# Moving matmul operands to other SBUF address remainders in a Mamba-2 mixer

## The chip, the cores and the metric

The kernel runs on one core of one Trainium2 chip. The metric is the device time of one execution in microseconds, of which the median over several runs is given. A profiled execution has a time of its own; its span is the time from its first to its last instruction.

## The reference, cut to what matters

One layer: RMSNorm of x (512 tokens, 2048 channels), a Mamba-2 mixer, a residual add and a final RMSNorm.

```python
proj = rmsnorm(x, ln_g) @ w_in             # 2048 -> 4096 z, 6144 x/B/C, 64 dt
xbc = silu(causal_depthwise_conv(xbc, conv_w, conv_b))
y = ssd_chunked_scan(xs * dt, dt * a, bm, cm) + d_skip * xs
y = rmsnorm(y * silu(z), norm_g)
out = rmsnorm(x + y @ w_out, final_g)      # 4096 -> 2048
```

Everything is float32, and most of the time goes into the two projections.

## The kernel before, in words

**Splitting.** TensorE works in a rounded float32. Each operand is therefore cut into a rounded high part and a low part (the rest), and a product is three matmuls: high by high, low by high, high by low. A weight piece is loaded from HBM (load_piece, line 78), ScalarE writes its high part (line 87) and VectorE its low part (line 88).

**Plain products.** The first eight output streams of the input projection are computed directly, in mm_k (lines 194 to 199). The weights are stationary. x in its high and low part is the moving operand, in two halves of 256 tokens. xh and xl hold all of x: 16 blocks of 128 channels by 512 tokens each, 32,768 bytes per partition. The squares of x and the splits of x run beside this.

**Quads.** The other 72 streams are taken in pairs, 36 quads, by a Strassen-like scheme with seven products in place of eight. It adds and subtracts quarters of the weights and of x. The quarters of the weights are combined by a DMA that adds (q_fetch) and by VectorE (q_add, line 604). The quarters of x are made once. Forms 1, 2 and 4 lie in the twelve tiles s0 to s11 (x_forms). Forms 11, 3, 12 and 22 are read from xh and xl in place, the second halves after x_form3 has rewritten them. operand() says where a form lies. product() (lines 627 to 636) issues the 24 matmuls of a product: line 634 high by high, 635 low part of x, 636 low part of the weights. pair() sets the order of the products: 11, 1, the 22 of the quad before, 4, 2, 12, 3.

**The scan.** Between the products TensorE also does the small float32 matmuls and transposes of the scan (lines 416 to 520), hung on steps of the matmul order in a table of events (ev). VectorE does the convolution and gating and ScalarE the exponentials. One quad in five is for the group matrices B and C, so the work repeats in groups of five quads. The results y go to HBM (yscr).

**Output projection.** Half of the blocks of w_out go directly (mm_o, lines 911 to 917): y is stationary and the weights are the moving operand, 512 columns. The others go in two groups by the same seven-product scheme: y_forms (lines 816 to 845) makes seven forms of y, each in a high and a low tile, f11h, f11l and so on; oproduct (lines 849 to 861) multiplies them. There the form of y is stationary and the weights are the moving operand. Line 859 is high by high, 860 the low part of y, 861 the low part of the weights. At the end the tiles of the seven forms are used a second time: last_piece (lines 940 to 946) puts seven of the last eight weight pieces into them, and the last loop (from line 1036) reads these as moving operands.

**Order of work.** The order on TensorE, SyncE and GpSimd is as written. ScalarE and VectorE are ordered by the tile framework, which also places the waits.

**Addresses.** The pools are stacks in each partition, handed out in steps of 32 bytes. The pools on the right side grow down from byte 229,344, and a tile "edge" of 32 bytes that holds nothing is their first. Below it lies the pool of x, 114,688 bytes, until the input projection is over: xh at 114,624, xl at 147,392, the twelve s tiles from 180,160 on. All of these leave the remainder 192 modulo 256. In the same place then comes the pool op: acc at 114,432, further tiles, and from 171,840 on the fourteen tiles of the seven forms, 4,096 bytes each, all at remainder 64. Two tiles that hold nothing, "gap" of 64 bytes ahead of them and "gap1" of 128 bytes behind them, shift them there. The weight tiles hi, lo, h1h and h1l on the left side, oh and ol, and the direct pieces of y (ya, yb, yc) are at remainder 0.

Of the kernel before, what the change touches and what calls it, by code (L numbers as in the profile page):

```python
# [10 lines left out]
F32 = mybir.dt.float32  # L11
F32R = mybir.dt.float32r
# [5 lines left out]
P = 128  # L18
L = 512
DM = 2048  # L20
KT = DM // P
# [13 lines left out]
def mamba_layer(ctx: ExitStack, tc: tile.TileContext, d: dict, out: bass.AP):  # L35
# [19 lines left out]
    xp = phx.enter_context(tc.tile_pool(name="xhat", bufs=1, side="right"))  # L55
# [23 lines left out]
    def load_piece(src, shape, name="ra"):  # L79
        raw = wp.tile(shape, F32, name=name, bufs=RB[name])  # L80
        nc.sync.dma_start(raw, src)
        return raw
# [42 lines left out]
    OSH = [P, 2, L]  # L125
# [12 lines left out]
    QSH = [P, 4, LH]  # L138
# [6 lines left out]
    def wo_src(p, s):  # L145
        return d["wo"][p // 2, s, :, p % 2 * 2:p % 2 * 2 + 2, :]
# [16 lines left out]
                                     *((op, ("oh", "ol")) if n % 4 == 3 else (wp,)))  # L163


    xh = xp.tile([P, KT, L], F32R, name="xh")
    xl = xp.tile([P, KT, L], F32R, name="xl")
    SSH = [P, 4, LH]
    xr = sp.tile([P, L + 48], F32, name="xr")

# [632 lines left out]
    yform = {}  # L803
# [3 lines left out]
    def y_fetch(i, j):  # L807

        yraw[i, j] = n1, n2 = [op.tile([P, 2, L], F32, name="yr", bufs=2) for _ in range(2)]
        for n, g in zip((n1, n2), oquads[i]):  # L810
            nc.sync.dma_start(n, yscr[g][:, 2 * j:2 * j + 2, :])
            for k in range(2):
                kk = 4 * g + 2 * j + k
                S.activation(n[:, k, :], n[:, k, :], AF.Identity, scale=ng[:, kk:kk + 1])

    def y_forms(i, j):

        n1, n2 = yraw.pop((i, j))
        if j == 0:
            if i == 0:  # L820
                op.tile([P, 16], F32, name="gap")
            for f in YF:
                yform[i, f] = [op.tile(QSH, F32R, name=f"f{f}{c}") for c in "hl"]
            if i == 0:
                op.tile([P, 32], F32, name="gap1")
        jj = slice(2 * j, 2 * j + 2)
        t = fp.tile([P, 2, 2, LH], F32, name="yt")
        t1, t2 = t[:, 0], t[:, 1]

        def put(f, t):  # L830
            hi, lo = [x[:, jj, :] for x in yform[i, f]]
            S.copy(out=hi, in_=t)
            V.tensor_tensor(out=lo, in0=t, in1=hi, op=ALU.subtract)

        put(11, n1[:, :, lo_])
        V.tensor_tensor(out=t1, in0=n2[:, :, hi_], in1=n1[:, :, hi_], op=ALU.subtract)
        put(1, t1)
        V.scalar_tensor_tensor(out=t2, in0=t1, scalar=-1.0, in1=n1[:, :, lo_], op0=ALU.mult, op1=ALU.subtract)
        V.tensor_tensor(out=n1[:, :, hi_], in0=n1[:, :, lo_], in1=n1[:, :, hi_], op=ALU.subtract)
        V.scalar_tensor_tensor(out=t1, in0=t2, scalar=-1.0, in1=n2[:, :, lo_], op0=ALU.mult, op1=ALU.subtract)  # L840
        put(4, t1)
        put(2, t2)
        put(12, n2[:, :, lo_])
        put(3, n1[:, :, hi_])
        put(22, n2[:, :, hi_])

    YF = (11, 1, 4, 2, 12, 3, 22)

    def oproduct(ps, i, w, f, first, step):

# [89 lines left out]
    def last_piece(i):  # L940

        raw = load_piece(wo_src(14 + i % 2, i // 2), OSH)
        hi, lo = [op.tile(OSH, F32R, name=f"f{YF[i]}{c}" if i < 7 else "o" + c) for c in "hl"]
        S.copy(out=hi, in_=raw)
        V.tensor_tensor(out=lo, in0=raw, in1=hi, op=ALU.subtract)
        wlast.append((hi, lo))

    m = 0
    for i, blk in enumerate(blocks):
        if type(blk) is tuple:  # L950
            for s in range(4):
                q_events(len(quads) + 4 * m + s, base[i] + s * QS, s == 3, 0, 3 if s == 0 else 0)
            for j in range(2):
                add(base[i] - ((50, 32), (54, 32))[m][j], y_fetch, m, j)
                add(base[i] - ((39, 24), (47, 24))[m][j], y_forms, m, j)
            m += 1
# [6 lines left out]
    for i in range(7):  # L963
        add(base[4] - QS + 5 + 5 * i, last_piece, i)
# [16 lines left out]
    op = ctx.enter_context(tc.tile_pool(name="op", bufs=1, side="right"))  # L981
# [5 lines left out]
    for kb, blk in enumerate(blocks[:-1]):  # L987
# [8 lines left out]
        for s, pairs in blk:  # L996
            ps = [None] * NC
            for p in pairs:
# [4 lines left out]
                for t in range(NC):  # L1003
# [8 lines left out]
                    if p == pairs[-1]:  # L1012
                        a = acc[:, t, s * L:(s + 1) * L]
# [19 lines left out]

    assert not ev, ev
    last_piece(7)
    for t in range(NC):
        ss = fp.tile([P, 4], F32, name="ss", bufs=2)
        for s in range(4):
            ps = ps_o.tile([P, L], F32, name="mm")
            for i in range(2):  # L1040
                mm_o(ps, wlast[2 * s + i], ys[14 + i], t, i == 0, i == 1)
            a = acc[:, t, s * L:(s + 1) * L]
# [4 lines left out]
                            op=ALU.mult)  # L1047
# [6 lines left out]
        n = 2 if t < NC - 1 else 4  # L1054
        for i in range(n):
            c = slice(i * (DM // n), (i + 1) * (DM // n))
# [41 lines left out]
```

## Time and profile before

| | |
|---|---|
| median of 3 runs | 1301.98 us (1300.03 to 1308.32) |
| profiled execution | 1302.64 us |
| its span | 1300.9 us, 24461 instructions |
| mean granted TensorE clock | 0.993 |
| moved by DMA | 225.90 MB, mean 174 GB/s |

How to read it: a row of a group names the line, the engine and the operation, output and inputs with their shapes and the count; then the total busy time in us and the mean of one in ns; then the idle time of the engine just before, with what ended it. The mean of a matmul is that of its whole passage through the pipelined array, so neighbouring matmuls overlap, and the distance from start to start is shorter than the mean. PE is TensorE's matmuls, PEld its weight loads. A view by stages gives the length of each stretch, then the busy time and count of each engine, the clock, the share of the DMA engines and GB/s.

### The profile page before, as it was taken

Reading aid. Unit: us, or ns where it says so; the run is one execution under the profiler, and the core shown is the slowest. Engines: PE = TensorE matmul, PEld = TensorE weight load, DVE = VectorE, ACT = ScalarE, POOL = GpSimd, SP = SyncE. Lnnn points to the kernel's source line nnn. Section 1 sums busy time; section 2 is a strip of 40 time slices with the busy share of each in tenths; the row PEclk is TensorE's granted clock in tenths of the full one; section 3 lists DMA queues with packets and bytes.
Section 4 is the critical chain, followed back from the end, with each engine's and each line's share of the span. In section 5 each row is a group of like instructions: output and inputs, shape, how many; then the busy total and the mean of one; then the engine's idle time right before and its main releaser. Section 6 shows DMA issues by size and latency. Waiting matters only on the chain.

```text
span 1300.9 us, 24461 instructions
## 1 busy us (share of the span) xinstructions
PE 1250.4 (96%) x9932; PEld 1188.6 (91%) x9932; DVE 1082.3 (83%) x1449; ACT 827.6 (64%) x1357; POOL 77.7 (6%) x99
## 2 busy tenths in 40 slices
PE   8989999999999999999999999999899899999997
PEld 7989899999999999999999999999888799789885
DVE  5796888989988998988899899889856887878865
ACT  7667667578666857766785777668655444534523
POOL 0000001010100101010000101010000000001000
PEclk9999999999999999999999999999999999999998
DMA  9546657575685667567566656756636677658612
GB/s 357 174 143 184 173 146 173 154 193 141 188 207 156 165 168 182 146 184 209 156 158 192 158 158 180 218 143 154 185 107 205 201 181 221 197 130 220 201 42 98
DMA packets 70194, 225.90 MB, mean 174 GB/s; under 512 B 8384, under 2 KB 12800, under 8 KB 69952
## 3 DMA queue, kind: packets, MB, share of 16 engines
q1 hardware_dynamic: 56688, 176.34, 40.5%
q0 software_dynamic: 12672, 46.14, 21.4%
q8 instruction: 78, 1.28, 0.4%
q10 hardware_dynamic: 720, 1.84, 0.4%
q14 instruction: 36, 0.29, 0.1%
HBM read 211.52 MB, written 12.78 MB: 172 GB/s over the span
## 4 chain that ended last, share of the span: by engine, by line
PE 59%; DVE 15%; DMA 11%; ACT 8%; issue 6%; SPq 0%; POOL 0%; DVEq 0%; ACTq 0%; POOLq 0%
PE S L636 5%; PE S L634 5%; PE S L635 5%; PE mm L859 3%; PE mm L634 3%; PE mm L860 3%; PE mm L915 3%; PE mm L861 3%; PE mm L917 3%; PE mm L916 3%; PE R L634 3%; PE R L635 3%; PE R L636 3%; DMA ra<-in_wi 3%; DVE lo L88 3%
## 5 line engine op out<-in xcount | busy, mean ns | idle before, releaser
L88 DVE TENSOR_TENSOR lo<-ra,hi 128x1024 fp32r<-128x1024 f32 x150 | 180.7, 1220 | 55.9 <-ACT hi L87 55.7
L87 ACT CAST hi<-ra 128x1024 fp32r<-128x1024 f32 x150 | 154.7, 1047 | 85.7 <-PE mm L860 19.7
L634 PE MATMUL mm<-xh,hi 128*128 128x256 f32 x576 | 163.8, 284 | 0.0
L634 PE MATMUL R<-s,hi 128*128 128x256 f32 x576 | 160.7, 279 | 2.6 <-ACT sn L656 2.6
L87 ACT CAST hi<-rc 128x1024 fp32r<-128x1024 f32 x94 | 98.4, 1047 | 101.0 <-DMA rc<-in_wi 58.5
L636 PE MATMUL mm<-xh,lo 128*128 128x256 f32 x576 | 160.7, 279 | 0.3 <-DVE lo L88 0.3
L635 PE MATMUL mm<-xl,hi 128*128 128x256 f32 x576 | 160.6, 279 | 0.0
L636 PE MATMUL R<-s,lo 128*128 128x256 f32 x576 | 160.2, 278 | 0.0
L635 PE MATMUL R<-s,hi 128*128 128x256 f32 x576 | 160.2, 278 | 0.0
L604 DVE TENSOR_TENSOR ra<-ra,rc 128x1024 f32<-128x1024 f32 x88 | 107.4, 1220 | 33.9 <-DMA rc<-in_wi 33.5
L88 DVE TENSOR_TENSOR lo<-rc,hi 128x1024 fp32r<-128x1024 f32 x94 | 114.5, 1218 | 0.9 <-ACT hi L87 0.8
L634 PEld LDWEIGHTS mm<-xh,hi 128*128 128x128 f32 x576 | 108.4, 188 | 5.1 <-issue 5.0
L634 PEld LDWEIGHTS R<-s,hi 128*128 128x128 f32 x576 | 108.2, 188 | 3.4 <-ACT sn L656 3.4
L636 PEld LDWEIGHTS mm<-xh,lo 128*128 128x128 f32 x576 | 109.3, 190 | 0.5 <-DVE lo L88 0.5
L636 PEld LDWEIGHTS R<-s,lo 128*128 128x128 f32 x576 | 109.0, 189 | 0.0
L635 PEld LDWEIGHTS mm<-xl,hi 128*128 128x128 f32 x576 | 108.5, 188 | 0.1
L635 PEld LDWEIGHTS R<-s,hi 128*128 128x128 f32 x576 | 108.2, 188 | 0.0
L634 PE MATMUL S<-xh,hi 128*128 128x256 f32 x288 | 81.4, 282 | 9.8 <-ACT sn L670 7.5
L636 PE MATMUL S<-xh,lo 128*128 128x256 f32 x288 | 82.2, 285 | 4.3 <-DVE lo L88 4.3
L634 PE MATMUL S<-xh,h1h 128*128 128x256 f32 x288 | 83.3, 289 | 1.0 <-ACT mm L676 1.0
L635 PE MATMUL S<-xl,hi 128*128 128x256 f32 x288 | 80.3, 279 | 0.7 <-DVE xl L578 0.7
L635 PE MATMUL S<-xl,h1h 128*128 128x256 f32 x288 | 80.6, 280 | 0.0
(452 smaller groups left out, 3929.2 us busy)
## 6 DMA issues: line engine op xcount, KB each, us to landing
rc<-in_wi SPq DMA_DIRECT2D x76, 512.0 KB, 5.3
ra<-in_wi SPq DMA_DIRECT2D x42, 512.0 KB, 6.1
rb<-in_wi SPq DMA_DIRECT2D x40, 512.0 KB, 7.5
ra<-in_wi POOLq DMA_DIRECT2D x36, 512.0 KB, 7.7
rb<-in_wi POOLq DMA_DIRECT2D x36, 512.0 KB, 6.4
csb<-cscr SPq DMA_DIRECT2D x32, 512.0 KB, 8.7
ra<-in_wo SPq DMA_DIRECT2D x26, 512.0 KB, 5.2
yscr<-xs SPq DMA_DIRECT2D x32, 256.0 KB, 2.7
```

What stands on the lines that cost most here:

```text
L87: S.copy(out=hi, in_=raw)
L88: V.tensor_tensor(out=lo, in0=raw, in1=hi, op=ALU.subtract)
L604: V.tensor_tensor(out=raw, in0=raw, in1=qs[n][other], op=ALU.add)
L634: T.matmul(ps, hi[:, k, :], ah, start=first and k == 0, stop=False, skip_group_check=True)
L635: T.matmul(ps, hi[:, k, :], al, start=False, stop=False, skip_group_check=True)
L636: T.matmul(ps, lo[:, k, :], ah, start=False, stop=k == KH - 1, skip_group_check=True)
L859: T.matmul(ps[:, t, :], yh[:, k, tt], hi[:, k, :], start=st, stop=False, skip_group_check=True)
L860: T.matmul(ps[:, t, :], yl[:, k, tt], hi[:, k, :], start=False, stop=False, skip_group_check=True)
L861: T.matmul(ps[:, t, :], yh[:, k, tt], lo[:, k, :], start=False, stop=en, skip_group_check=True)
L915: T.matmul(ps, yh, hi, start=first and k == 0, stop=False)
L916: T.matmul(ps, yh, lo, start=False, stop=False)
L917: T.matmul(ps, yl, hi, start=False, stop=last and k == 1)
```

## The change

xh and xl become one tile of 65,568 bytes, 32 more than both. Each half lies 16 bytes behind the place it would have at the tile's start. The tile starts at 114,592 (remainder 160), so both halves leave the remainder 176; the s tiles stay where they were. Each form of y becomes one tile for its high and its low part. Six of the seven tiles are 32 bytes longer, with an inner offset of 16 bytes (8 bytes for form 2); form 4 has none. gap and gap1 are taken out. The pool op keeps its size, so the other tiles stay. The forms start at 171,776 (remainder 0) and leave the remainders 16, 48, 64, 72, 112, 144 and 176 in the order f11, f1, f4, f2, f12, f3, f22. In the last stage the weight pieces in these tiles have the same remainders. No instruction is added or removed.

```diff
-    xh = xp.tile([P, KT, L], F32R, name="xh")
-    xl = xp.tile([P, KT, L], F32R, name="xl")
+    xhl = xp.tile([P, 2 * KT * L + 8], F32R, name="xh")
+    xh, xl = [xhl[:, i * KT * L + 4:(i + 1) * KT * L + 4].rearrange("p (k l) -> p k l", k=KT) for i in range(2)]
...
+    def y_tile(f, shape):
+        n, o = shape[1] * shape[2], YF[f]
+        t = op.tile([P, 2 * n + (8 if o else 0)], F32R, name=f"f{f}")
+        return [t[:, i * n + o:(i + 1) * n + o].rearrange("p (a b) -> p a b", a=shape[1]) for i in range(2)]
...
         if j == 0:
-            if i == 0:
-                op.tile([P, 16], F32, name="gap")
             for f in YF:
-                yform[i, f] = [op.tile(QSH, F32R, name=f"f{f}{c}") for c in "hl"]
-            if i == 0:
-                op.tile([P, 32], F32, name="gap1")
+                yform[i, f] = y_tile(f, QSH)
...
-    YF = (11, 1, 4, 2, 12, 3, 22)
+    YF = {11: 4, 1: 4, 4: 0, 2: 2, 12: 4, 3: 4, 22: 4}
...
-        hi, lo = [op.tile(OSH, F32R, name=f"f{YF[i]}{c}" if i < 7 else "o" + c) for c in "hl"]
+        hi, lo = y_tile(list(YF)[i], OSH) if i < 7 else [op.tile(OSH, F32R, name="o" + c) for c in "hl"]
```

## The prediction, on record before the result

> **What bounds the kernel now.** I read the page first: the busy shares and the chain that ended last.
>
> ```profile
> span 1300.9 us, 24461 instructions
> PE 1250.4 (96%) x9932; PEld 1188.6 (91%) x9932; DVE 1082.3 (83%) x1449; ACT 827.6 (64%) x1357; POOL 77.7 (6%) x99
> PE 59%; DVE 15%; DMA 11%; ACT 8%; issue 6%; SPq 0%; POOL 0%; DVEq 0%; ACTq 0%; POOLq 0%
> ```
>
> TensorE is nearly always busy, yet the chain that set the end runs on it for only 59%; the rest is feeding. The change adds and removes no instruction, so it can only act through what one matmul costs. So I went to the timeline of TensorE in two quads of the x stage, first and last row of twelve matmuls in a row.
>
> ```profile
> 309.92 0.28 PE L634 MATMUL R<-s,hi 128*128 128x256 f32 x1
> ...
> 311.21 0.28 PE L636 MATMUL mm<-xh,lo 128*128 128x256 f32 x1
> ...
> 331.74 0.28 PE L634 MATMUL R<-s,hi 128*128 128x256 f32 x1
> ...
> 332.98 0.28 PE L636 MATMUL R<-s,lo 128*128 128x256 f32 x1
> ```
>
> From start to start it is 1.29 us / 11 = 117 ns in the first stretch and 1.24 us / 11 = 113 ns in the second, at the same remainders: moving operand at 192 modulo 256, weights at 0. In the first stretch the moving tile changes from the form s to xh without a change of pitch. So there are **two paces**, and remainder alone does not choose. The view by stages, restricted to line 635, tells them apart over whole quads (columns: stretch, length, TensorE busy and count, weight-load busy and count, clock, DMA):
>
> ```profile
> 304.90:327.60 22.70, 15.73 (x56) 10.52 (x56) 1.00 0.64 158
> 327.60:349.70 22.10, 15.47 (x56) 10.52 (x56) 1.00 0.70 197
> 643.30:666.00 22.70, 15.73 (x56) 10.52 (x56) 1.00 0.65 176
> 666.00:688.10 22.10, 15.48 (x56) 10.52 (x56) 1.00 0.64 172
> 869.70:892.40 22.70, 15.73 (x56) 10.52 (x56) 1.00 0.65 165
> 892.40:914.50 22.10, 15.47 (x56) 10.52 (x56) 1.00 0.74 182
> ```
>
> A slow quad has 15.73/56 = 280.9 ns per matmul, a fast one 276.3; the 4.6 ns are about the difference of the paces, and I use **4.5 ns** per matmul. The clock is 1.00 in all, so it is no throttle. The same quad of three different groups takes the same pace: what a stretch runs at is settled when TensorE starts again after another kind of work, and then it holds. The rows of all such matmuls give the mix:
>
> ```profile
> L635 PE MATMUL R<-s,hi 128*128 128x256 f32 x576 | 160.2, 278 | 0.0
> L635 PE MATMUL mm<-xl,hi 128*128 128x256 f32 x576 | 160.6, 279 | 0.0
> L198 PE MATMUL mm<-xl,hi 128*128 128x256 f32 x96 | 19.1, 280 | 0.0
> ```
>
> (160.2 + 160.6)/1152 = 278.5 ns, so (278.5 - 276.3)/4.6 = **about 0.47 of the x products run slow**; of the early plain products (line 198) about 0.8. For the output stage, line 860 by stages:
>
> ```profile
> 1017.20:1026.60 9.40, 6.74 (x24) 4.60 (x24) 1.00 0.39 60
> 1039.20:1094.90 55.70, 45.22 (x164) 30.72 (x164) 1.00 0.67 177
> ```
>
> 280.8 ns in the first, 275.7 in the second: slow at the entry, fast for the long rest; I call 0.15 of it slow.
>
> **The change part by part.** *Addresses.* Worked out from the tiles' sizes, xh and xl go from remainder 192 to 176 while the twelve form tiles of x stay at 192. The output's forms go from 64 to 16 (f11), 48 (f1), 64 (f4), 72 (f2), 112 (f12), 144 (f3), 176 (f22). acc, ya, hi, lo and the rest do not move. The two tiles gap and gap1 hold no work: 0 us.
>
> *One tile in place of two.* The high and low part now become free together, so a reallocated f tile waits for the later of the two last readers. In oproduct these are line 861 (high part) and line 860, one matmul earlier: at most 0.1 us for the low part, which waits for ScalarE's high part in any case. In last_piece the same:
>
> ```profile
> L945 DVE TENSOR_TENSOR f11l<-ra,f11h 128x1024 fp32r<-128x1024 f32 x1 | 1.2, 1227 | 0.1
> L945 DVE TENSOR_TENSOR f2l<-ra,f2h 128x1024 fp32r<-128x1024 f32 x1 | 1.2, 1218 | 0.0
> ```
>
> The wait stands on VectorE ahead of the next split, whose reader is a matmul some products later; 0 us. For xh and xl the last reader is the high part's, line 636 of the last product: 0 us.
>
> *VectorE and ScalarE at odd places.* xr is read and written 12 bytes past a boundary of 32 already, so the rows show what such a start costs them:
>
> ```profile
> L398 DVE TENSOR_TENSOR xr<-mm,rbc 128x512 f32<-128x512 f32 x39 | 26.8, 688 | 18.7 <-PE mm L636 15.7 <-PE mm L198 2.9
> L681 DVE TENSOR_TENSOR z<-z,rbc 128x512 f32<-128x512 f32 x30 | 20.5, 683 | 0.2
> L577 ACT CAST xh<-xr 128x512 fp32r<-128x512 f32 x4 | 2.5, 618 | 1.9 <-DVE xr L576 1.8
> L832 ACT CAST f12h<-yr 128x512 fp32r<-128x512 f32 x4 | 2.5, 618 | 0.0
> ```
>
> 688 ns against 683 (one reads PSUM, the other does not) and 618 against 618: 5 ns at most for each of some 90 splits, 0.5 us, hidden since TensorE reads the result later. I take 0.
>
> *TensorE's paces.* No matmul of this kernel that counts in the sum has an operand at 16, 48, 72, 112, 144 or 176, so this cost is bounded from both sides by the two paces.
> - x products: 36 quads of 7 x 24 matmuls, 6048. All fast saves 6048 x 0.47 x 4.5 ns = 12.8 us of TensorE; all slow costs 6048 x 0.53 x 4.5 = 14.4. Four of seven products read the moved halves; since a pace carries over from tile to tile, I let the bound hold all.
> - Plain products: 8 x 16 x 6 = 768. Down 768 x 0.8 x 4.5 = 2.8, up 0.7.
> - Output products: 1344. Down 0.9, up 1344 x 0.85 x 4.5 = 5.1.
> - Last stage: the f tiles hold weights of the output projection there and are the moving operand, 168 matmuls:
>
> ```profile
> L915 PE MATMUL mm<-f1h,ych 128*128 128x512 f32 x8 | 3.2, 394 | 0.0
> L916 PE MATMUL mm<-f1l,ych 128*128 128x512 f32 x8 | 3.1, 388 | 0.0
> L917 PE MATMUL mm<-f1h,ycl 128*128 128x512 f32 x8 | 3.1, 392 | 0.0
> L915 PE MATMUL mm<-oh,ybh 128*128 128x512 f32 x24 | 9.3, 389 | 0.0
> ```
>
> The mean of the three is 391.3 against 389 at remainder 0, which is the one sign in the trace that a remainder matters: 168 x 2.3 ns = 0.4 us either way.
>
> *What of it reaches the end.* Quad by quad all of it: 22.70 against 22.10 us, both with TensorE always busy. Over groups of five quads hardly any (columns: length, then busy TensorE, weight loads, VectorE, ScalarE, POOL):
>
> ```profile
> 281.20:394.30 113.10, 110.95 (x961) 107.93 (x960) 99.84 (x130) 79.33 (x136) 8.62 (x10) 1.00 0.67 177
> 394.30:507.20 112.90, 110.89 (x960) 107.83 (x959) 99.26 (x129) 79.10 (x136) 8.65 (x10) 1.00 0.65 170
> 507.20:619.60 112.40, 110.26 (x960) 107.13 (x959) 99.70 (x130) 79.05 (x136) 8.60 (x10) 1.00 0.68 178
> 619.60:733.50 113.90, 111.41 (x962) 108.16 (x960) 99.69 (x129) 78.94 (x136) 8.61 (x10) 1.00 0.64 168
> 733.50:846.10 112.60, 111.22 (x961) 108.44 (x959) 99.89 (x130) 79.20 (x136) 8.62 (x10) 1.00 0.67 178
> ```
>
> The third group has 0.96 us less matmul time than the fifth and is only 0.20 us shorter. What a fast quad gains is waited for in the last quad of its group, where the chain runs over loads and splits:
>
> ```profile
> 604.67 10.20 DMA ra<-in_wi
> ...
> 708.71 9.37 DMA csb<-cscr
> ```
>
> So what is late next when TensorE is faster are these transfers. I take **half** for x and plain products (between 0.20/0.96 = 0.2 and 1), all of the output and last stages: over 1039 to 1095 us TensorE is busy in every slice (9 in the page) and nothing there absorbs a change.
>
> *The sum.* The profiled execution took 1302.64 us (span 1300.9 and 1.74 around it), 0.66 above the median 1301.98. x products: four boundaries per quad now shift the moving operand by 16 bytes, each a new chance to fall into either pace; at 0.47 before I see no side, 0 (ends -12.8 x 0.5 and +14.4 x 0.5). Plain products, 0.8 slow now, to 0.47: 768 x 0.33 x 4.5 = 1.1, half of it, -0.6. Output products: 0, nearer to the long fast stretch. Last stage: -0.2. Together -0.8: 1301.8 for such an execution, less the 0.66, **1301.2 us**.
>
> The Trainium skill bears on this twice. "SBUF — State Buffer", section "Who interferes with whom", says that PE has two independent read ports and never waits on anyone; by that the two paces could not come from its reads and all terms would be 0, 1302.0 us. The rows of line 635 show two paces that it leaves unexplained. The same page, "Specifications (TRN2)", gives 16-byte lines with a penalty for each new one; f2 at 72 crosses 33 instead of 32 per weight row. If that stretched its 192 weight loads of 188 ns by 1/32, an estimate from that page, the sum would be 1.1 us higher; no row here shows it.
>
> **The rivals.**
> 1. *The addresses do nothing at all*; paces stay as they fall: 1302.0. For it: both paces at the same remainder. Against it: the last stage's 391.3 against 389.
> 2. *The fast lock.* Breaking the common remainder of x keeps TensorE out of the slow pace: (12.8 + 2.8) / 2 + 0.9 + 0.4 = 9.1, so 1302.0 - 9.1 = 1292.9; passing wholly, 16.9 saved, 1285.1. For it: the output stage held the fast pace for 55.7 us. Against it: that was at a difference of 192 between moving operand and weights, the same as in the slow quads.
> 3. *The slow lock* (the other side). Operands that start 16 bytes off put a conflict into every stretch, in x's products and the output's alike: (14.4 + 0.7) / 2 + 5.1 + 0.4 = 13.1, so 1315.1; wholly, 20.6, 1322.6. It decides as soon as more than about half of the x products run slow. For it: the f tiles at 64 are the slower ones in the last stage. Against it: nothing puts 176 nearer to that than 192.
>
> **How the numbers follow.** Forecast (mixed paces, shifted) 0.50; rival 1 0.14; rival 2 0.22; rival 3 0.14. About 1% is what a measurement of this kernel can tell from no change, 1289.0 to 1315.0. Of rival 2 rather more than half falls above 1289.0, as much as halving does; 0.10 below, and a pace faster than any row shows has another 0.03 out of the forecast's share: faster 0.13. Of rival 3 half is over 1315.0: slower 0.07; within 1% 0.80. The range reaches to 1289.0 in rival 2 and to 1312.0 in rival 3: about 0.13 and 0.08 are left out. Sign: rivals 2 and 3 nearly cancel; the forecast's own range is 1297 to 1306.
>
> **What would show it.** Line 635's time per matmul by quads: between 276.3 and 280.9 in a mixture, changing now within a quad where the moving tile changes from s to xh; all at 276 with rival 2, all at 281 or above with rival 3. The groups of five quads should stay within 112 and 114 us whatever the pace; if TensorE's busy time falls by 10 us or more and the span by as much, the half was wrong. VectorE's and ScalarE's split durations should stand still (618, 683, 1220 ns). A pace below 113 ns per 256 columns, or one well above 118, would make the bounds themselves wrong.

## The result and the profile after

The changed kernel took 1313.66 us (median of 8 runs, 1311.45 to 1317.11), beside 1303.06 us for the kernel before (8 runs, 1295.3 to 1308.32). The ratio is 1.0081, with a 95% interval of 1.006 to 1.0102: about 10.6 us slower. The forecast was 1301.2 us with a range from 1289.0 to 1312.0.

The profiled execution took 1315.43 us. Its page, span and busy line:

```profile
span 1313.6 us, 24461 instructions
PE 1269.3 (97%) x9932; PEld 1209.3 (92%) x9932; DVE 1083.4 (82%) x1449; ACT 827.4 (63%) x1357; POOL 77.6 (6%) x99
```

The span is 12.7 us longer. The instructions are the same in number, and VectorE, ScalarE and GpSimd are as busy as before (1082.3, 827.6, 77.7). TensorE alone has more: 18.9 us of matmul and 20.7 us of weight load. The view by stages shows where. Before, with the plain products, the quads, the direct output products, the output products by forms, and the last stage:

```profile
0.00:120.90 120.90, 109.44 (x864) 106.18 (x865) 88.34 (x146) 84.14 (x135) 3.64 (x13) 0.99 0.64 220
120.90:948.20 827.30, 806.64 (x6913) 782.22 (x6912) 725.22 (x934) 577.38 (x986) 60.30 (x70) 1.00 0.65 171
948.20:1017.20 69.00, 69.00 (x336) 56.89 (x336) 47.51 (x73) 44.58 (x73) 0.86 (x1) 1.00 0.55 179
1017.20:1228.20 211.00, 201.97 (x1549) 191.54 (x1548) 174.81 (x206) 97.35 (x118) 12.91 (x15) 1.00 0.69 188
1228.20:1300.90 72.70, 63.39 (x279) 51.73 (x277) 46.39 (x92) 24.17 (x47) 0.00 (x0) 0.95 0.22 82
```

The same stages after:

```profile
0.00:123.20 123.20, 112.28 (x863) 108.80 (x864) 88.53 (x146) 84.04 (x135) 3.63 (x13) 0.99 0.62 216
123.20:958.20 835.00, 816.27 (x6912) 792.73 (x6911) 725.35 (x934) 577.25 (x986) 60.23 (x70) 0.99 0.65 169
958.20:1027.30 69.10, 69.10 (x338) 56.95 (x336) 47.73 (x73) 44.42 (x73) 0.85 (x1) 1.00 0.56 179
1027.30:1240.50 213.20, 207.89 (x1549) 199.07 (x1548) 175.51 (x206) 97.79 (x118) 12.89 (x15) 0.99 0.68 186
1240.50:1313.60 73.10, 63.79 (x279) 51.78 (x277) 46.28 (x92) 23.84 (x47) 0.00 (x0) 0.95 0.22 81
```

The lengths grow by 2.3, 7.7, 0.1, 2.2 and 0.4 us, which makes the 12.7. The stage whose operands did not move, the third, stands still. The granted clock is 0.99 to 1.00 in all stages but the last in both, so it explains nothing. In the groups of matmuls, after:

```profile
L635 PE MATMUL mm<-xh,hi 128*128 128x256 f32 x576 | 163.5, 284 | 0.0
L635 PE MATMUL R<-s,hi 128*128 128x256 f32 x576 | 159.7, 277 | 0.0
L198 PE MATMUL mm<-xh,hi 128*128 128x256 f32 x192 | 31.0, 284 | 0.0
L916 PE MATMUL mm<-f,ybh 128*128 128x512 f32 x32 | 12.6, 393 | 0.0
L577 ACT CAST xh<-xr 128x512 fp32r<-128x512 f32 x4 | 2.5, 618 | 1.8 <-DVE xr L576 1.6
L946 DVE TENSOR_TENSOR f<-ra,f 128x1024 fp32r<-128x1024 f32 x7 | 8.6, 1224 | 2.5 <-ACT f L945 2.4
```

(The tile of both halves bears the name xh, so the first row is the group mm<-xl of before. From the output stage on, lines are one higher.) Line 635 on the moved halves went from 279 to 284 ns. The same line on the s tiles, which stayed at 192, went from 278 to 277. The splits that write to the odd places stand at 618 and 1224 ns.

The timeline of TensorE shows the pace inside one quad. The first two rows are 15 matmuls apart, the next two 3 apart:

```profile
333.98 0.28 PE L634 MATMUL S<-xh,h1h 128*128 128x256 f32 x1
...
335.77 0.28 PE L634 MATMUL S<-xh,h1h 128*128 128x256 f32 x1
...
338.88 0.28 PE L634 MATMUL R<-s,hi 128*128 128x256 f32 x1
...
339.22 0.28 PE L634 MATMUL mm<-xh,hi 128*128 128x256 f32 x1
```

1.79 us / 15 = 119 ns on the moved half, 0.34 / 3 = 113 on an s tile. Before, a stretch held one pace from restart to restart, whatever tile it read; now the pace follows the tile. The mean by whole quads, which the prediction named as the thing to look at, hides this. Line 635 in two neighbouring quads after:

```profile
311.00:333.50 22.50, 15.72 (x56) 10.52 (x56) 1.00 0.61 158
333.50:356.00 22.50, 15.72 (x56) 10.52 (x56) 1.00 0.72 199
```

15.72/56 = 280.7 ns in both, nearly the slow quad's 280.9 of before. But it is the mean of 284 on the halves and 277 on the s tiles, in the ratio of four to three.

So I took the distance from start to start for all neighbouring matmuls out of the trace (distances over 145 ns, which hold a wait, left out), by the tile and by **the difference of the two addresses: start of the moving operand less start of the weights, modulo 256**:

```
256 columns                     before: difference, mean ns     after: difference, mean ns
plain products (xh, xl moving)  192  117.0                      176  119.3
quads, xh and xl                192  115.5                      176  119.3
quads, s tiles                  192  115.4                      192  114.1
output, f11 f1 f4 f2            192  114.4 114.5 114.1 113.4    240 208 192 184  118.3 118.3 117.4 118.3
output, f12 f3 f22              192  113.3 113.4 114.0          144 112 80       119.9 118.6 118.1
512 columns
last stage, f tiles moving      64   229.2                      16 to 176        230.5 to 233.2
last stage, others              0    227.2 to 227.6             0                227.0 to 227.5
```

At 192, means between 113.3 and 117.8 are mixtures of the two known paces. At every other difference for 256 columns the mean in this table is 118.1 or more. (Form 4 stays at 192 after the change; its 117.4 is discussed below.) Counting what lies above 113.33 ns (226.67 for 512 columns) gives TensorE's **excess**: 16.7 us in the execution before, 33.6 after. That is 16.9 us more, in one execution of each kernel; their spans differ by 12.7.

### The profile page after: what moved, and what is told of

The parts are those of the page before. It is cut to its first block, busy times and chain, and to the rows that moved or that the text cites. A ratio compares the mean times of both kernels' runs of the same rounds, so it can differ in the third digit from the quotient of the medians.

```text
span 1313.6 us, 24461 instructions
## 1 busy us (share of the span) xinstructions
PE 1269.3 (97%) x9932; PEld 1209.3 (92%) x9932; DVE 1083.4 (82%) x1449; ACT 827.4 (63%) x1357; POOL 77.6 (6%) x99
## 4 chain that ended last, share of the span: by engine, by line
PE 59%; DVE 14%; DMA 6%; issue 4%; ACT 3%; SPq 0%; DVEq 0%; ACTq 0%
PE S L636 4%; PE S L634 4%; PE S L635 4%; PE mm L916 4%; PE mm L917 4%; PE mm L918 4%; PE mm L860 4%; PE mm L862 4%; PE mm L861 4%; DMA rc<-in_wi 3%; PE mm L634 3%; PE R L634 3%; PE R L635 3%; PE R L636 3%; PE mm L635 2%
## 5 line engine op out<-in xcount | busy, mean ns | idle before, releaser
L634 PE MATMUL mm<-xh,hi 128*128 128x256 f32 x576 | 165.0, 287 | 0.0
L635 PE MATMUL mm<-xh,hi 128*128 128x256 f32 x576 | 163.5, 284 | 0.0
L634 PEld LDWEIGHTS mm<-xh,hi 128*128 128x128 f32 x576 | 108.3, 188 | 5.0 <-issue 5.0
L860 PE MATMUL mm<-hi,f 128*128 128x256 f32 x384 | 109.1, 284 | 4.0 <-DVE acc L897 2.2
L862 PE MATMUL mm<-lo,f 128*128 128x256 f32 x384 | 108.8, 283 | 1.4 <-DVE lo L88 1.4
L861 PE MATMUL mm<-hi,f 128*128 128x256 f32 x384 | 108.6, 283 | 0.0
L635 PEld LDWEIGHTS mm<-xh,hi 128*128 128x128 f32 x576 | 108.2, 188 | 0.0
```

Source lines behind the costliest of these rows:

```text
L634: T.matmul(ps, hi[:, k, :], ah, start=first and k == 0, stop=False, skip_group_check=True)
L635: T.matmul(ps, hi[:, k, :], al, start=False, stop=False, skip_group_check=True)
L860: T.matmul(ps[:, t, :], yh[:, k, tt], hi[:, k, :], start=st, stop=False, skip_group_check=True)
L861: T.matmul(ps[:, t, :], yl[:, k, tt], hi[:, k, :], start=False, stop=False, skip_group_check=True)
L862: T.matmul(ps[:, t, :], yh[:, k, tt], lo[:, k, :], start=False, stop=en, skip_group_check=True)
```

## The experiments

The theory that the table suggests: a matmul has another pace, and not the fast one, where its two operands lie at another distance from each other than 192, modulo 256. Its rivals: the addresses count one by one and not against each other; a coarser step (64 bytes) is what breaks the good case; the merged tiles cause waits; the output's part and not x's is the cost. A ratio compares a version with the kernel before as measured in the same series, whose median lay between 1303.55 and 1304.71 us.

**x alone.** The kernel before with the tile of x changed, and nothing else.

```diff
-    xh = xp.tile([P, KT, L], F32R, name="xh")
-    xl = xp.tile([P, KT, L], F32R, name="xl")
+    xhl = xp.tile([P, 2 * KT * L + 8], F32R, name="xh")
+    xh, xl = [xhl[:, i * KT * L + 4:(i + 1) * KT * L + 4].rearrange("p (k l) -> p k l", k=KT) for i in range(2)]
```

> Only x's halves move (176), the output's forms stay at 64. Granule theory (an operand of TensorE that starts off a multiple of 64 bytes costs some 6 ns in each matmul, whatever stands beside it): plain products and those of xh and xl 119 ns from start to start, those of the s tiles 114, output products 114 as before; about 5 to 7 us over the kernel before. Difference theory (what counts is moving minus stationary remainder, 176 here): the same paces. Merging theory (one tile for two parts adds waits): the cost is not in the pace, and half of the 10.6 us stays at most.

Measured: 1310.78 us (1307.27 to 1316.85), ratio 1.0061 [1.0039, 1.0083]. Its groups:

```profile
L635 PE MATMUL mm<-xh,hi 128*128 128x256 f32 x576 | 163.5, 284 | 0.0
L635 PE MATMUL R<-s,hi 128*128 128x256 f32 x576 | 159.4, 277 | 0.0
```

The same two rows as in the changed kernel, to 0.3 us. About three quarters of the loss (0.61 of 0.81%) come from x.

**The output's forms alone.** The kernel before with y_tile and YF, without gap and gap1.

```diff
+    YF = {11: 4, 1: 4, 4: 0, 2: 2, 12: 4, 3: 4, 22: 4}
...
-                yform[i, f] = [op.tile(QSH, F32R, name=f"f{f}{c}") for c in "hl"]
+                yform[i, f] = y_tile(f, QSH)
```

> Only the output's forms move (16 to 176), x stays at 192. Granule theory: output products 118 ns, but those of form 4, which is still at 64, only as long as they follow a form off 64; x products 115.4 in a mix of 113 and 118; 4 to 6 us over the kernel before. Difference theory: each form of its own, some at 113. Merging theory: the paces stay at 114.

Measured: 1307.96 us (1303.23 to 1309.61), ratio 1.0018 [1.0001, 1.0035]. The group of line 635 on xl, and the output stage as a whole:

```profile
L635 PE MATMUL mm<-xl,hi 128*128 128x256 f32 x576 | 160.4, 278 | 0.0
```

```profile
1020.50:1234.20 213.70, 208.04 (x1548) 199.01 (x1547) 176.13 (x207) 98.47 (x118) 12.89 (x15) 0.99 0.67 186
```

x's products are as before. The output stage has 6.1 us more of matmul than before (208.04 against 201.97) and is 2.7 us longer. The loss is 2.4 us where 4 to 6 were expected. The two parts, 0.61% and 0.18%, add up to the 0.81% of the whole within their intervals.

**One tile, old addresses.** The changed kernel with the halves of x back at 192 and all forms back at 64 (gap and gap1 put in again), still one tile for two parts.

```diff
-    xhl = xp.tile([P, 2 * KT * L + 8], F32R, name="xh")
-    xh, xl = [xhl[:, i * KT * L + 4:(i + 1) * KT * L + 4]...
+    xhl = xp.tile([P, 2 * KT * L + 16], F32R, name="xh")
+    xh, xl = [xhl[:, i * KT * L + 16:(i + 1) * KT * L + 16]...
...
-    YF = {11: 4, 1: 4, 4: 0, 2: 2, 12: 4, 3: 4, 22: 4}
+    YF = {11: 0, 1: 0, 4: 0, 2: 0, 12: 0, 3: 0, 22: 0}
```

> One tile for two parts everywhere, all remainders as before (x 192, forms 64). Granule and difference theory: 1303, within 3 us of the kernel before, and the two paces in a mix. Merging theory: 1311 or more.

Measured: 1303.93 us (1300.92 to 1307.23), ratio 0.9991 [0.9973, 1.001]. Merging two tiles into one costs nothing within 0.3%; the addresses carry the loss. Line 635 on the halves of x:

```profile
L635 PE MATMUL mm<-xh,hi 128*128 128x256 f32 x576 | 160.0, 278 | 0.0
```

**x at 128.** As x alone, but both halves 64 bytes before the old place.

```diff
...
+    xhl = xp.tile([P, 2 * KT * L + 16], F32R, name="xh")
+    xh, xl = [xhl[:, i * KT * L + 0:(i + 1) * KT * L + 0]...
```

> x's halves at 128, a multiple of 64 other than the s tiles' 192. Granule theory: no cost, paces 113 and 118 only, 1298 to 1305. Difference theory: a pace of its own for xh and xl, other than that of the s tiles; up to 1315 if it is as bad as 176.

Measured: 1308.29 us (1304.81 to 1312.68), ratio 1.0021 [1.0004, 1.0038].

```profile
L635 PE MATMUL mm<-xh,hi 128*128 128x256 f32 x576 | 162.0, 281 | 0.0
L635 PE MATMUL R<-s,hi 128*128 128x256 f32 x576 | 159.7, 277 | 0.0
```

The halves run at 118.7 ns (plain products 119.4), the s tiles at 114.2. A shift by a whole 64 bytes loses the fast pace too, so the idea that only the place within 64 bytes matters falls. The loss of time is only a third of that with x alone, though the paces (118.7 and 119.3 ns on the halves) are close; why so little of it reaches the end is not known.

**A scan of places.** The kernel before with empty tiles in x's pool, so that xh and xl lie at 0 and the forms 1, 2 and 4 at 32, 96 and 160; in a second kernel xh, xl and form 4 at 64, form 2 at 224 and form 1 at 192.

```diff
+    PADS = {0: 32, 4: 64, 8: 64, 12: 32}
...
+    def pad(k2):
+        if PADS.pop(k2, 0):
+            xp.tile([P, PADW[k2]], F32, name=f"pad{k2}")
...
```

({0: 128, 4: 32, 8: 96, 12: 128} in the second)

> Empty tiles move x's halves to remainder 0 and the forms of x to 32 (form 1), 96 (form 2) and 160 (form 4); weights stay at 0. The 64-byte granule theory is out since x at 128 costs as much as at 176. Difference theory: each difference between moving and stationary remainder has a pace of its own, 113 to 124 ns; 0 should be the fast one, since the 512-column runs at 0 hold 227, and the others 117 to 120. Same-as-forms theory (the pace suffers whenever consecutive products differ in remainder, whatever it is): all four at 117 or more, also 0. Time between 1303 and 1325.

> Empty tiles move x's halves and form 4 to 64 and form 2 to 224, form 1 stays at 192. Difference theory: 64 above 117 in both, 224 a pace of its own, form 1 at 113 to 114 as in the changed kernel. Same-as-forms theory: form 1 suffers as well, 117 or more. Time between 1303 and 1325.

Measured, one execution each: 1313.61 us and 1309.06 us, beside a median of 1304.71 for the kernel before (1299.9 to 1310.37, so that the second lies inside its range). Start to start in the first: 119.7 at 0, 118.0 at 32, 119.7 at 96, 117.4 at 160. In the second: 117.6 at 64, 118.2 at 224, and 114.4 at 192, the only mean of the seven under 117. Place 0 was expected to be fast, as it is for 512 columns, and was not. Form 1 at 192 kept its pace among neighbours at 64, so it is not enough for a loss that consecutive products differ in place. In the groups of the first (lines are 10 higher):

```profile
L645 PE MATMUL mm<-xl,hi 128*128 128x256 f32 x576 | 162.9, 283 | 0.0
L645 PE MATMUL R<-s,hi 128*128 128x256 f32 x576 | 160.9, 279 | 0.0
L645 PE MATMUL S<-s,hi 128*128 128x256 f32 x288 | 81.1, 282 | 0.0
```

The rows on s tell that tiles at other remainders now pay like x: 282 ns for form 2 at 96, against 276 in the changed kernel at 192.

The mean of 117.6 at 64 in the second kernel is no new pace. Nearly all of the 178 products there that can be followed ran at 117.8 ns, but six ran at 113.3, one of them here, rows 12 matmuls apart (1.36 us / 12 = 113 ns):

```profile
262.83 0.28 PE L644 MATMUL S<-xh,hi 128*128 128x256 f32 x1
...
264.19 0.28 PE L644 MATMUL S<-xh,h1h 128*128 128x256 f32 x1
```

So 64 has the two paces of 192, the fast one seldom. At no other difference did any product in these traces run at it.

**Everything 32 bytes on.** The kernel before without "edge" and with 32 empty bytes at the start of the left side: x at 224, weights at 32, the forms of y at 96. All differences stay, all remainders change.

```diff
-    edge = ctx.enter_context(tc.tile_pool(name="edge", bufs=1, side="right"))
-    edge.tile([P, 8], F32, name="edge")
...
+    const.tile([P, 8], F32, name="lpad")
```

> All tiles of both sides lie 32 bytes higher, so that x is at 224 and the weights at 32, the output's forms at 96: every address changes, every difference stays. Difference theory: 113 and 118 in a mix, 1303 within 3 us. Absolute theory (some remainders are bad in themselves, 192 and 0 are good): another pace, most likely 118 and more, and 1310 or above.

Measured: 1304.66 us (1300.64 to 1309.47), ratio 0.9992 [0.9971, 1.0014]. Start to start 115.0 to 115.4 in the x stage and 113.5 to 114.2 in the output stage, mixtures of 113 and 118 as before. Line 635 (634 here):

```profile
L634 PE MATMUL mm<-xl,hi 128*128 128x256 f32 x576 | 160.2, 278 | 0.0
L634 PE MATMUL R<-s,hi 128*128 128x256 f32 x576 | 160.1, 278 | 0.0
```

No remainder of the operands themselves survived here, and nothing was lost. **The difference decides** which paces a matmul can take, not the two addresses by themselves.

**Only the weights 32 bytes on.** The counterpart: "lpad" is put in and "edge" stays. x stays at 192, the weights go to 32.

```diff
+    const.tile([P, 8], F32, name="lpad")
```

> The left side alone lies 32 bytes higher: weights at 32, x and its forms at 192 as before, so the difference of all x products is 160. Difference theory: what x at 160 with weights at 0 gave (117.4 ns in form 4), now for plain products, halves and forms alike, and no stretch at 113. Absolute theory is already out by the kernel with everything 32 higher.

Measured: 1312.38 us, beside 1297.73 for the kernel before, one run each. (The latter is low among that kernel's runs; against its usual median the loss is some 9 us.) Line 635 (636 here):

```profile
L636 PE MATMUL R<-s,hi 128*128 128x256 f32 x576 | 161.6, 281 | 0.0
L636 PE MATMUL mm<-xl,hi 128*128 128x256 f32 x576 | 161.5, 280 | 0.0
```

x was not touched, yet all its products run at 117.9 ns (difference 160) and the output's at 118.3 (224): every 256-column product lost the 113 ns, the s tiles too. The scan of places had these two differences from other addresses, 160 with 117.4 and 224 with 118.2, so two placements of each agree within 0.5 ns. The excess is 41.0 us, the largest of all.

**Four bytes off.** As x alone, with the halves at 188 and at 196.

```diff
+    xhl = xp.tile([P, 2 * KT * L + 16], F32R, name="xh")
+    xh, xl = [xhl[:, i * KT * L + 15:(i + 1) * KT * L + 15]...
```

(and 64 and 1 in the place of 16 and 15 for 196)

> x's halves at 188, 4 bytes short of 192. If the fast pace hangs on a difference of 192 exactly (or on whole 16-byte lines): plain products 117 to 120. If 192 is the edge or the middle of a band: 113, perhaps without the slow alternative, and 5 to 10 us less than the kernel before.

> x's halves at 196, 4 bytes past 192. As for 188: 117 to 120 if 192 counts exactly, 113 if it lies in a band that reaches upward.

Measured, one execution each: 1308.39 and 1314.76 us, beside the same single 1297.73; the first lies inside the range that the kernel before has elsewhere. Start to start on the halves 116.6 at 188 (plain products 119.7) and 120.3 at 196 (122.0, the slowest mean for 256 columns in this study). Four bytes to either side of 192 are enough to lose the 113 ns. But 188 is not simply slow: 107 of 141 products on the halves ran near 115.6 ns, between the two paces of 192, and the others near 120. The 512-column products with x moving and weights at 192, one run of 32, disagree about the two sides: 227.0 at 188 (difference 252), 236.7 at 196 (difference 4), and 227.5 at difference 0.

**The scan's tiles moved.** To learn whether the scan's float32 work settles which of the two paces a restart takes, the pool of the scan was shifted by 64 and by 128 bytes in the kernel before.

```diff
+    sp.tile([P, 16], F32, name="spad")
```

(32 in the place of 16 for the second)

> x, weights and the output's forms as before (difference 192); only the scan's own tiles lie 64 bytes higher, 0 in place of 192. Between two quads TensorE comes from these tiles. Difference theory alone: paces 113 and 118 in a mix as before, 1303 within 3 us. If what ran just before settles which of the two paces a stretch falls into, the mix shifts: from all at 113 (8 us less) to all at 118 (10 us more).

> As the kernel with 64, with the scan's tiles 128 bytes higher, at 64. The same two outcomes; a mix other than in both the kernel before and the one with 64 would show that the entry can be chosen by addresses of other work.

Measured: 1301.90 us (1298.23 to 1305.09), ratio 0.9986 [0.9966, 1.0005], and 1304.3 us (1299.34 to 1306.07), ratio 1.0 [0.998, 1.0021]. Two stages of the first, the quads and the output products by forms:

```profile
120.30:946.50 826.20, 802.68 (x6912) 777.60 (x6911) 725.72 (x934) 577.24 (x987) 60.20 (x70) 0.99 0.65 171
...
1015.60:1227.60 212.00, 205.70 (x1550) 195.91 (x1549) 175.66 (x207) 97.69 (x118) 12.89 (x15) 0.99 0.67 187
```

Against before the quads have 4.0 us less of matmul time (802.68 against 806.64) and are only 1.1 us shorter; the output products took 3.7 us more and are 1.0 us longer, although no operand of theirs moved. So the mixture of the two paces is not the same in each kernel, also where no operand moved. With one execution of each traced, it stays open whether the place of the scan's tiles shifts it or whether it differs between executions. No version here is faster than the kernel before by more than its interval.

## Why the prediction was wrong

**The step that failed** is "TensorE's paces", in the sentence "so this cost is bounded from both sides by the two paces", with its term in the sum, "x products: ... I see no side, 0". The trace of before held two paces at one difference, 192, and I concluded that "remainder alone does not choose". The evidence allowed only this: at 192 two paces occur. Nothing in it said that another difference has the fast one as often, or that it is no slower than the slow one. All 256-column rows of before stood at the same difference; the only rows elsewhere were the 512-column ones, 391.3 against 389 at 64 instead of 0, and I valued them at 0.4 us. They were the one sign that the difference matters.

Measured against the terms, as excess and as length of the stage:
- *x products*: forecast 0. The moved halves cost 12.4 us more (6.98 to 19.36 us of excess), a mean of 119.3 where the bound was 118. The s tiles gave back 3.4 (5.37 to 1.95). Together +9.0; the stage is 7.7 us longer. Of the 12.4 some 7.5 are the lost fast pace (115.5 to 117.8 ns over 3,320 matmuls) and some 5 the pace beyond the slow one (117.8 to 119.3). The 9.0 stay under the bound of 14.4: what failed first here is the "no side, 0", and only then the bound.
- *Plain products*: forecast -0.6. Excess 2.6 to 4.2 us; the stage is 2.3 us longer.
- *Output products*: forecast 0. Excess 0.7 to 6.7 us, 5.9 more where the bound was 5.1; the stage is 2.2 us longer.
- *Last stage*: forecast -0.2. Excess 0.42 to 0.87 us; 0.4 us longer.

**"A pace carries over from tile to tile"** held before and fell with the change. In the trace before, of 119 stretches of eight matmuls or more in the x stage 71 ran at the fast pace throughout, 47 at the slow one, and one changed, behind a gap of 140 ns. After, 88 of 107 changed, at the borders between xh or xl and an s tile, and none was fast throughout. This was the first sign that the prediction named, "changing now within a quad", and it was there. The other, a pace "well above 118", as well, with 119.3 ns: it "would make the bounds themselves wrong", and it did. The mean by quads alone would have misled: 280.7 in each quad looked at is nearest to the sign of rival 3, "all at 281 or above". Carrying over remains where both neighbours allow it. Form 4, unmoved at 192, ran fast in seven of its eight products before and slow in seven of eight after, most of them behind form 22 at another difference. Its tile in the last stage, unmoved at 64, took 228.9 ns before and 232.0 after, between tiles at 48 and 72. So what runs next to a matmul seems to count beside its own difference; no run was made for this alone.

**What reaches the end.** The half for x's products is neither borne out nor refuted: 7.7 of 9.0 us here, 3.3 of 8.5 with x alone, 4.3 of 14.6 with the weights moved, from one execution each. The one with x alone was the fastest of its ten, 1307.27 us against a median of 1310.78. "All of the output" was wrong: 2.2 of 5.9 us, and 2.7 of 5.9 with the forms alone. The stretch from 1039 to 1095 us was read rightly as leaving no room; before:

```profile
1039.20:1094.90 55.70, 55.70 (x494) 55.70 (x493) 47.33 (x53) 26.55 (x30) 4.22 (x5) 1.00 0.67 177
```

But it is only a quarter of the stage. Over the whole stage TensorE was idle for 211.00 - 201.97 = 9.0 us before and 5.3 after, and these 3.7 us took the rest.

The groups of five quads, after:

```profile
287.00:401.30 114.30, 111.89 (x960) 109.05 (x959) 99.74 (x130) 79.19 (x136) 8.62 (x10) 1.00 0.67 175
401.30:515.30 114.00, 112.12 (x962) 109.07 (x960) 99.42 (x129) 79.29 (x136) 8.66 (x10) 1.00 0.65 168
515.30:628.90 113.60, 112.07 (x961) 109.02 (x959) 99.68 (x130) 78.97 (x136) 8.58 (x10) 1.00 0.67 174
628.90:743.30 114.40, 112.09 (x962) 109.04 (x959) 99.66 (x128) 79.03 (x136) 8.62 (x10) 1.00 0.64 168
743.30:855.70 112.40, 111.54 (x961) 108.89 (x959) 99.60 (x130) 79.13 (x136) 8.58 (x10) 1.00 0.67 174
```

Together they have 4.98 us more of matmul than before (559.71 against 554.73) and are 3.8 us longer; two are over the 114 us that the prediction gave as their limit.

**What was right.** One tile in place of two is 0 (ratio 0.9991 [0.9973, 1.001]). The splits at odd places stand still. The first rival, addresses that do nothing, is excluded; so is the fast lock.

**The slow lock**, to which I gave 0.14, had the right side and nearly the time, 1315.1 us for 1313.66. But its mechanism is not what was seen. It let every product run at the slow pace, s tiles included, with 7.2 us of its 13.1 from x and 5.1 from the output. In fact the moved halves run slower than that pace, the s tiles faster than before, and the output passes on less than half. That the time came out so near was luck. Its text said "Operands that start 16 bytes off put a conflict into every stretch"; "nothing puts 176 nearer to that than 192" was the weak sentence, since 192 was the one difference of which the trace showed the fast pace.

The Trainium skill, "SBUF — State Buffer", section "Who interferes with whom", has PE's two read ports independent and PE waiting on nobody. The kernel with everything shifted (115 ns) and the one with only the weights shifted (118 ns) differ only in where the right side begins, and so in the distance between TensorE's two operands. By that rule, read as saying that TensorE's two reads cannot slow each other, they would be equal. They are not; whether the reads are what collides, no run here shows. The estimate of 1.1 us for a form at 72, from the same page's "Specifications (TRN2)", is not borne out: f2 at 72 runs at 118.3 ns like f11 at 16, in both kernels that have it, and its weight loads took 188.7 ns in the changed kernel against 188.2 at 16 and 189.7 at 48.

**Open.** What it is that collides, how a neighbour acts on the next product, why the good difference is 192 for 256 columns and 0 for 512, why 64 has the fast pace seldom, and what picks one of the two paces at a restart, none of these runs tells. The paces off 192 (116.6 to 122.0) follow no order that I could find. The excess is counted in one execution of each kernel, and the mixture at 192 differs among the kernels traced, so single us of it should not be read.

## What to carry to other kernels

Where TensorE is the bound, compare the distance from start to start between groups whose operands differ only in address, and sort them by the difference of the two addresses, not by each one alone. Before a tile is shifted, ask what every other operand that meets it does: shifting both sides together by 32 bytes cost nothing here (ratio 0.9992 [0.9971, 1.0014]), while shifting one made the matmuls that it met 1 to 4% longer (from a mean of 115.5 ns to between 116.6 and 120.3). And two values seen at one setting are no bounds for another setting; where the trace holds only one, leave the range open to the side that was never seen.

## What was not expected of the hardware

- A 128x128 by 256 matmul followed the one before it after 113 or 118 ns where its moving operand lay 192 bytes, modulo 256, beyond its weights (three placements: 192 and 0, 0 and 64, 224 and 32), and after 116.6 to 122.0 ns on average at sixteen other differences, from 0 to 240. At 64 the fast pace still occurred, in 6 of 178 products.
- Four bytes matter: 116.6 to 119.7 ns at 188 (most products on the halves near 115.6, the others near 120), 120.3 to 122.0 at 196.
- With 512 columns the good difference was 0 (227 ns, with both operands at 0, 32, 192 or 224), and 252 did as well (227.0); 4 took 236.7, 192 took 233.1 and 233.5, and 240 took 235.7 (all but the 227 at 0 from runs of 32 matmuls).
- Weight loads lengthen along with it, from 1188.6 to 1209.3 us in sum, at the same count.
